# Attention's value product as fp32r parts: values' rounded and rest columns side by side as one 128-column operand, probabilities split in two

## The chip, the cores and the metric

The kernel runs on one core of a Trainium2 chip. The metric is the device time of one execution in microseconds (us), the median of three runs; smaller is better. The engines are PE (TensorE, matrix products), DVE (VectorE), ACT (ScalarE), POOL (GpSimd) and SP (SyncE, which issues the transfers). Each works through its own queue in order, and semaphores hold an instruction back until what it needs is there. SBUF is the memory on the chip, PSUM the memory that PE writes its products to.

## What is computed

The reference is two layers of a decoder trunk over 1024 positions with 1024 features, in fp32. A layer normalises its input, projects it, runs three groups of heads on the projection (sliding-window attention, an HGRN2 recurrence, a gated delta rule), projects their joined outputs, and then runs a SwiGLU feed-forward network (FFN). Each of the two halves of a layer is a residual that is scaled, shifted and gated by a modulation computed from a second input. Cut to the attention that the change touches:

```
kb, vb = band(k), band(v)          # this block of 128 positions and the one before
scores = jnp.einsum('bnqhgd,bnkhd->bnhgqk', qb, kb).astype(jnp.float32) * (d ** -0.5)
scores = jnp.where(valid[None, :, None, None], scores, -jnp.inf)   # causal, within 128 positions
m = jnp.maximum(scores.max(axis=-1, keepdims=True), sink)
p = jnp.exp(scores - m)
denom = p.sum(axis=-1, keepdims=True) + jnp.exp(sink - m)
out = jnp.einsum('bnhgqk,bnkhd->bnqhgd', (p / denom).astype(v.dtype), vb)
```

There are eight query heads in two groups that share a key and a value head each, with 64 features to a head.

## The kernel before

**Dense products.** All large products (input projection `p_fm` and `p_tm`, output projection `o_ps`, FFN `gu_ps` and `dn_ps`) go through `mm3`: both operands are split in a rounded part and a rest (`hhi`/`hlo`, `whi`/`wlo`), and three fp32r matmuls of 512 columns (256 for `p_tm`) make the product. They stream on PE nearly without a stop. For each weight piece a transfer lands, ACT rounds it (line 770) and DVE subtracts to get the rest (line 771). fp32r is the type of a matmul's operands that were rounded when written.

**Halves and mixers.** The 1024 positions are two halves of 512, each a sequence of four blocks of 128. A mixer is the work of the three head groups on one half of one layer: `gdn` (gated delta rule), `hgrn` and `attention`. They are Python generators, and `Weaver` takes the next step of the one that is least advanced. `Pace` puts such steps between the dense matmuls: each `mm3` ticks a clock, credit builds up at a rate, a step costs one credit, and a generator that yields a number is left alone until so many us of that clock have passed. So `yield 2.5` behind the probabilities' work says how much dense work shall stand between the transposes and the product. `end_m` runs whatever steps are left without a pause. Four mixers run: (layer 0, half 0) beside the projection of half 1, the three others beside FFN stages. Behind `end_m(0, 0)` comes the first output projection, which needs everything that the first mixer wrote.

**Attention in a block.** For each block, keys and queries are normalised, rotated, split and transposed (`pk`, `pq`). Then, for each of the two key/value heads g (a "group" here; 32 in all, 4 of them in a first block that has no block before it): eight score products `psc`, a softmax in `sc` (DVE lines 336 to 352, ACT lines 345 and 354), and four transposes that bring the probabilities to PSUM as `pt`. They are used twice: masked for this block as `ptc` and for the block before as `ptp` (POOL's affine_select, lines 360 and 364, which zeroes what lies outside the window), each behind an ACT copy from PSUM (lines 359 and 363). The value product is plain fp32:

```
og = po[64 * g:64 * g + 64].rearrange("p a b -> p (a b)")
T.matmul(og, k.vring[:, cur, 64 * g:64 * g + 64], ptc.rearrange("p a b -> p (a b)"),
         start=True, stop=first)
```

and the same on line 371 with `ptp` and the block before. `vring` holds the values of two blocks, copied by POOL on line 268. The profile names the slot of SBUF that `sc`, `ptc` and `ptp` lie in `scr`, and counts two records for each of these fp32 matmuls.

**The start.** `build_consts` fills mask constants (`mc`) on POOL in a scratch tile, and DVE casts them to `mcr` on line 101; `hgrn` uses them from its first block on. While they are made, the modulation's products run on DVE and POOL (lines 1172 and 1175, tile `adag`, with the tag "gt"), and the first pieces of the input projection begin on PE (`first_pieces`: `hhi` from ACT line 1150, `hlo` from DVE line 1151).

The scheduler of the framework sets the order of instructions on each engine from priorities and from when buffers come free, so a change of a few steps moves many rows.

## Time and profile before

| | us |
|---|---|
| median of 3 runs | 2741.18 (2739.95 to 2748.74) |
| the profiled execution | 2744.08 |
| its span in the profile | 2742.4 |
| PE busy | 2616.8 (95% of the span) |
| DVE busy | 1869.8 (68%) |
| ACT busy | 1158.3 (42%) |
| POOL busy | 377.9 (14%) |

The span is the time from the first to the last instruction of the profiled execution. An engine's share is an average over stages: where PE is busy throughout, the other engines' work is hidden; where it isn't, something else sets the time.

### The profile page before, as it was taken

The numbers are of one execution on the slowest core, as the hardware profiler recorded it, in microseconds if no ns is written. First come the engines' busy times: TensorE is split into PE (matmuls) and PEld (weight loads), VectorE is DVE, ScalarE is ACT, GpSimd is POOL, SyncE is SP. The second block draws the span as 40 slices with busy tenths as digits, with TensorE's granted clock in tenths as the row PEclk, the third lists the DMA queues.
The fourth block names the chain that finished last, engine by engine and source line by source line (L and its number), as shares of the span: only waits on it lengthen the run. The fifth ranks groups of instructions, "written<-read, shape, count | busy, mean of one in ns | idle before, by whom it ended". The sixth has DMA issues, their size and how long they took to land.

```text
span 2742.4 us, 42796 instructions
## 1 busy us (share of the span) xinstructions
PE 2616.8 (95%) x15488; PEld 2117.0 (77%) x15488; DVE 1869.8 (68%) x4863; ACT 1158.3 (42%) x2434; POOL 377.9 (14%) x560
## 2 busy tenths in 40 slices
PE   4989898899999999999999999999999999999999
PEld 3887776777777778887877777898787777788887
DVE  7679886777968567567887757637777854544444
ACT  4636573333445444433344444543344544322222
POOL 6132210402101001311011001211110100100000
PEclk9999999999999999999999999999999999999999
DMA  6644336543333355544433335452332224333323
GB/s 234 195 149 132 115 100 205 167 123 91 122 114 101 110 166 160 181 124 135 128 99 105 108 124 178 134 156 74 98 114 88 70 76 154 117 93 95 93 80 108
DMA packets 171956, 343.96 MB, mean 125 GB/s; under 512 B 20832, under 2 KB 80480, under 8 KB 171744
## 3 DMA queue, kind: packets, MB, share of 16 engines
q1 hardware_dynamic: 170880, 341.16, 40.0%
q8 instruction: 122, 2.00, 0.3%
q14 instruction: 90, 0.74, 0.1%
q10 hardware_dynamic: 864, 0.07, 0.0%
HBM read 299.15 MB, written 42.01 MB: 124 GB/s over the span
## 4 chain that ended last, share of the span: by engine, by line
PE 67%; DVE 17%; issue 5%; POOL 4%; ACT 4%; DMA 2%; SPq 0%; POOLq 0%; ACTq 0%; DVEq 0%
PE gu_ps L799 10%; PE gu_ps L800 9%; PE gu_ps L801 9%; PE dn_ps L799 5%; PE dn_ps L800 5%; PE dn_ps L801 5%; DVE wlo L771 3%; PE p_tm L800 2%; PE p_tm L801 2%; PE p_tm L799 2%; PE o_ps L800 2%; PE o_ps L801 2%; PE o_ps L799 2%; POOL n_xn L850 1%; PE pl L484 1%
## 5 line engine op out<-in xcount | busy, mean ns | idle before, releaser
L770 ACT ACTIVATE whi<-wraw 128x1024 fp32r<-128x1024 f32 (+3 forms) x484 | 422.9, 875 | 788.9 <-PE gu_ps L800 240.6
L771 DVE TENSOR_TENSOR wlo<-wraw,whi 128x1024 fp32r<-128x1024 f32 (+3 forms) x484 | 493.3, 1020 | 271.1 <-ACT whi L770 261.3
L799 PE MATMUL gu_ps<-hhi,whi 128*128 128x512 f32 x1408 | 572.4, 407 | 3.4 <-DVE n_xn L848 2.6
L800 PE MATMUL gu_ps<-hlo,whi 128*128 128x512 f32 x1408 | 559.8, 398 | 0.8 <-DVE hlo L852 0.7
L801 PE MATMUL gu_ps<-hhi,wlo 128*128 128x512 f32 x1408 | 560.2, 398 | 0.0
L799 PEld LDWEIGHTS gu_ps<-hhi,whi 128*128 128x128 f32 x1408 | 267.4, 190 | 74.0 <-issue 13.9
L801 PEld LDWEIGHTS gu_ps<-hhi,wlo 128*128 128x128 f32 x1408 | 266.1, 189 | 61.6 <-issue 0.8
L800 PEld LDWEIGHTS gu_ps<-hlo,whi 128*128 128x128 f32 x1408 | 266.6, 189 | 58.1 <-DVE hlo L852 2.8
L799 PE MATMUL dn_ps<-gt,whi 128*128 128x512 f32 x704 | 287.6, 410 | 2.0 <-DVE xt L1061 1.3
L800 PE MATMUL dn_ps<-gt,whi 128*128 128x512 f32 x704 | 278.5, 396 | 0.4 <-DVE gt L1049 0.4
L801 PE MATMUL dn_ps<-gt,wlo 128*128 128x512 f32 x704 | 277.5, 394 | 0.0
L799 PE MATMUL p_tm<-whi,hhi 128*128 128x256 f32 (+1 forms) x896 | 255.7, 286 | 6.7 <-ACT cx L875 3.5
L800 PE MATMUL p_tm<-wlo,hhi 128*128 128x256 f32 (+1 forms) x896 | 256.2, 286 | 5.8 <-DVE wlo L771 5.8
L801 PE MATMUL p_tm<-whi,hlo 128*128 128x256 f32 (+1 forms) x896 | 254.7, 284 | 0.0
L799 PEld LDWEIGHTS p_tm<-whi,hhi 128*128 128x128 f32 x896 | 170.3, 190 | 9.6 <-ACT cx L875 4.3
L800 PEld LDWEIGHTS p_tm<-wlo,hhi 128*128 128x128 f32 x896 | 170.3, 190 | 9.1 <-DVE wlo L771 7.5
L801 PEld LDWEIGHTS p_tm<-whi,hlo 128*128 128x128 f32 x896 | 170.1, 190 | 1.9 <-issue 1.6
L799 PEld LDWEIGHTS dn_ps<-gt,whi 128*128 128x128 f32 x704 | 132.3, 188 | 37.8 <-issue 7.6
L1061 DVE SCALAR_TENSOR_TENSOR xt<-dn_ps,gth,xt 128x512 f32<-128x512 f32 x144 | 107.8, 748 | 77.1 <-PE dn_ps L801 76.7
L801 PEld LDWEIGHTS dn_ps<-gt,wlo 128*128 128x128 f32 x704 | 132.3, 188 | 31.0
L800 PEld LDWEIGHTS dn_ps<-gt,whi 128*128 128x128 f32 x704 | 132.5, 188 | 30.6 <-DVE gt L1049 4.4
L1046 DVE TENSOR_TENSOR g_t<-g_t,gu_ps 128x512 f32<-128x512 f32 x88 | 60.2, 685 | 119.0 <-PE gu_ps L801 118.6
(409 smaller groups left out, 4436.3 us busy)
## 6 DMA issues: line engine op xcount, KB each, us to landing
wraw<-in_w_gate_dram SPq DMA_DIRECT2D x88, 512.0 KB, 3.7
wraw<-in_w_up_dram SPq DMA_DIRECT2D x88, 512.0 KB, 4.0
wraw<-in_ada_w_dram SPq DMA_DIRECT2D x80, 512.0 KB, 3.7
wraw<-in_w_down_dram SPq DMA_DIRECT2D x128, 256.0 KB, 2.7
wraw<-in_w_in_t_dram SPq DMA_DIRECT2D x48, 512.0 KB, 4.0
wraw<-in_w_in_f_dram SPq DMA_DIRECT2D x32, 512.0 KB, 4.0
wraw<-in_w_out_dram SPq DMA_DIRECT2D x32, 512.0 KB, 4.0
wraw<-in_w_down_dram SPq DMA_DIRECT2D x64, 192.0 KB, 2.4
```

Source lines behind the costliest of these rows:

```text
L484: T.matmul(pl[r][cols, li, p, :], lh, rh, start=True, stop=True)
L770: nc.scalar.activation(hi[:, 0:n], raw[:, 0:n], AF.Copy)
L771: nc.vector.tensor_tensor(out=lo[:, 0:n], in0=raw[:, 0:n], in1=hi[:, 0:n].bitcast(F32), op=ALU.subtract)
L799: T.matmul(out, lh, rh, start=first, stop=False)
L800: T.matmul(out, lh, rl, start=False, stop=False)
L801: T.matmul(out, ll, rh, start=False, stop=last)
L850: nc.gpsimd.tensor_scalar(out=xn, in0=xn, scalar1=acol[:, i:i + 1], scalar2=bcol[:, i:i + 1], op0=ALU.mult, op1=ALU.add)
L1046: V.tensor_tensor(out=t, in0=t, in1=pss[1], op=ALU.mult)
L1061: V.scalar_tensor_tensor(out=x, in0=ps, scalar=k.gth[l][:, m:m + 1], in1=x, op0=ALU.mult, op1=ALU.add)
```

## The change

Values are kept twice, as their rounded part (ACT copy) and the rest (DVE subtraction), side by side: for a head, `vring[:, cur, g]` has 2 x 64 columns. Probabilities likewise: `ptc[:, 0]` is the rounded copy that ACT makes from PSUM, `ptc[:, 1]` what DVE leaves by subtracting it. POOL masks both parts for both blocks, four selects where there were two (two for one in a first block). The product is four fp32r matmuls (two in a first block) that add up in one PSUM tile `po`, whose upper 64 rows belong to the rounded values and whose lower 64 to the rest; an ACT copy and a DVE addition join them into the output tile `a_ot`. Further: `po` is taken for each group rather than for both, `yield 2.5` becomes `yield 4.5`, a `yield 1.0` follows the products and a `yield 0.0` goes; attention's input tile is single, and the next block's transfer is issued behind the normalisation. To make room, the slots of scratch are handed out in halves (class `Slot`, `half`), `hgrn`'s `h_ld` is cut to half and its first half lies in such a half slot, and the mask constants' scratch is a tile of the pool `gp` with the tag "gt", taken behind the first step of `build_consts`.

```diff
@@ -66,9 +66,7 @@
     nc, tc = k.nc, k.tc
     cp = k.const
     G, V = nc.gpsimd, nc.vector
-    t1 = k.mp.tile([128, 1024], F32, name="h_ld")
     t2 = k.mp.tile([128, 6, 128], F32, name="cv").rearrange("p a t -> p (a t)")
-    mc = t1.rearrange("p (l t) -> p l t", l=NL + 1)
     idt = t2[:, 640:768]
     mk, mk2 = t2[:, 0:128], t2[:, 128:192]
     e, ef = t2[:, 192:320].bitcast(I32), t2[:, 320:448]
@@ -83,6 +81,7 @@
     k.ones = cp.tile([128, 128], F32, name="ones")
     G.memset(k.ones, 1.0)
     yield
+    mc = k.gp.tile([128, 1024], F32, name="mct", tag="gt").rearrange("p (l t) -> p l t", l=NL + 1)
 
     def sel(ap, pattern, base, cm):
         G.affine_select(out=ap, in_=ap, pattern=pattern, compare_op=ALU.is_ge, fill=0.0,
@@ -189,7 +188,7 @@
         nc.scalar.activation(k.sin2[:, :, j, :], ang, AF.Sin)
         nc.scalar.activation(k.cos2[:, :, j, :], nn, AF.Sin)
     k.kring = cp.tile([128, 4, 2, 128], F32R, name="kring")
-    k.vring = cp.tile([128, 2, 128], F32, name="vring")
+    k.vring = cp.tile([128, 2, 2, 2, 64], F32R, name="vring")
     k.sB = cp.tile([128, 2, 128], F32, name="sB")
     k.sC = cp.tile([128, 2, 128], F32, name="sC")
 
@@ -246,26 +245,25 @@
     qs = mp.tile([128, 4, 2, 64], F32R, name="a_qs")
     qT = mp.tile([128, 4, 128], F32R, name="a_qT")
     ks = mp.tile([128, 2, 2, 2, 64], F32R, name="a_ks")
-    sc = r2[:, 1024:1536].rearrange("p (a t) -> p a t", a=4)
-    ptc = r2[:, 1536:2048].rearrange("p (a t) -> p a t", a=4)
-    ptp = r2[:, 2048:2560].rearrange("p (a t) -> p a t", a=4)
-    qk = r2[:, 0:640].rearrange("p (h d) -> p h d", d=64)
+    r2, pf = r2
+    at = r2[:, 0:768]
+    qk = r2[:, 768:1408].rearrange("p (h d) -> p h d", d=64)
+    sc = r2[:, 1408:1920].rearrange("p (a t) -> p a t", a=4)
+    ptc, ptp = (pf[:, 2 * i:2 * i + 2].rearrange("p u (a t) -> p u a t", a=4) for i in range(2))
     sq = mp.tile([128, 10, 64], F32, name="a_sq")
     def load(b):
-        at = r2[:, 2560 + 768 * (b % 2):3328 + 768 * (b % 2)]
         nc.sync.dma_start(out=at, in_=tmr[b, :, 0:768])
-        return at
-
-    nxt = load(0)
+
+    load(0)
     yield 3.0
     for b in range(NB):
         gb = NB * h + b
         cur = gb % 2
         first = gb == 0
-        at = nxt
-        if b + 1 < NB:
-            nxt = load(b + 1)
-        G.tensor_copy(k.vring[:, cur, :], at[:, 640:768])
+        av = at[:, 640:768].rearrange("p (g d) -> p g d", g=2)
+        A.activation(k.vring[:, cur, :, 0, :], av, AF.Copy)
+        V.tensor_tensor(out=k.vring[:, cur, :, 1, :], in0=av, in1=k.vring[:, cur, :, 0, :].bitcast(F32),
+                        op=ALU.subtract)
         a3 = at[:, 0:640].rearrange("p (h d) -> p h d", d=64)
         A.activation(sq, a3, AF.Square)
         ss = k.small.tile([128, 10], F32, name="a_ss")
@@ -280,6 +278,8 @@
             V.scalar_tensor_tensor(out=qk[:, 8 + j, :], in0=a3[:, 8 + j, :],
                                    scalar=rs[:, 8 + j:9 + j], in1=lc.gq[:, 1, :],
                                    op0=ALU.mult, op1=ALU.mult)
+        if b + 1 < NB:
+            load(b + 1)
         xr = qk[:, :, 0:16]
         pc = sq[:, 0:3, :].rearrange("p a d -> p (a d)")[:, 0:160].rearrange("p (h d) -> p h d", d=16)
         ps_ = sq[:, 3:6, :].rearrange("p a d -> p (a d)")[:, 0:160].rearrange("p (h d) -> p h d", d=16)
@@ -308,7 +308,7 @@
         A.activation(k.kring[:, :, cur, :], pk, AF.Copy)
         den = k.small.tile([128, 8], F32, name="a_den")
         yield 0.5
-        po = k.pb.tile([128, 4, 128], F32, name="po", tag="b")
+        ot = mp.tile([128, 4, 128], F32, name="a_ot", tag="fo")
         for g in range(2):
             pq = k.pb.tile([128, 4, 128], F32R, name="pq", tag="b")
             for j in range(4):
@@ -356,24 +356,26 @@
             pt = k.pb.tile([128, 4, 128], F32, name="pt", tag="b")
             for j in range(4):
                 T.transpose(pt[:, j, :], sc[:, j, :], k.ident)
-            A.activation(ptc, pt, AF.Copy)
-            G.affine_select(out=ptc, in_=ptc, pattern=[[0, 4], [1, 128]],
-                            compare_op=ALU.is_ge, fill=0.0, base=0, channel_multiplier=-1)
-            if not first:
-                A.activation(ptp, pt, AF.Copy)
-                G.affine_select(out=ptp, in_=ptp, pattern=[[0, 4], [-1, 128]],
-                                compare_op=ALU.is_gt, fill=0.0, base=0, channel_multiplier=1)
-            yield 2.5
-            og = po[64 * g:64 * g + 64].rearrange("p a b -> p (a b)")
-            T.matmul(og, k.vring[:, cur, 64 * g:64 * g + 64], ptc.rearrange("p a b -> p (a b)"),
-                     start=True, stop=first)
-            if not first:
-                T.matmul(og, k.vring[:, 1 - cur, 64 * g:64 * g + 64],
-                         ptp.rearrange("p a b -> p (a b)"), start=False, stop=True)
-            if g == 0:
-                yield 0.0
-        ot = mp.tile([128, 4, 128], F32, name="a_ot", tag="fo")
-        A.activation(ot, po, AF.Copy)
+            A.activation(ptc[:, 0], pt, AF.Copy)
+            V.tensor_tensor(out=ptc[:, 1], in0=pt, in1=ptc[:, 0].bitcast(F32), op=ALU.subtract)
+            for u in range(2):
+                pu = ptc[:, u].bitcast(F32)
+                if not first:
+                    G.affine_select(out=ptp[:, u], in_=pu, pattern=[[0, 4], [-1, 128]],
+                                    compare_op=ALU.is_gt, fill=0.0, base=0, channel_multiplier=1)
+                G.affine_select(out=ptc[:, u], in_=pu, pattern=[[0, 4], [1, 128]],
+                                compare_op=ALU.is_ge, fill=0.0, base=0, channel_multiplier=-1)
+            yield 4.5
+            po = k.pb.tile([128, 4, 128], F32, name="po", tag="b")
+            pof = po.rearrange("p a b -> p (a b)")
+            terms = [(v, t, u) for v, t in ((cur, ptc), (1 - cur, ptp))[:1 if first else 2] for u in range(2)]
+            for i, (v, t, u) in enumerate(terms):
+                T.matmul(pof, k.vring[:, v, g].rearrange("p a b -> p (a b)"), t[:, u].rearrange("p a b -> p (a b)"),
+                         start=(i == 0), stop=(i == len(terms) - 1))
+            yield 1.0
+            rows = slice(64 * g, 64 * g + 64)
+            A.activation(ot[rows], po[0:64], AF.Copy)
+            V.tensor_tensor(out=ot[rows], in0=ot[rows], in1=po[64:128], op=ALU.add)
         nc.sync.dma_start(out=mixr[:, 0:4, 128 * b:128 * b + 128], in_=ot)
         yield 0.0
 
@@ -419,24 +421,25 @@
     V, A, G, T = nc.vector, nc.scalar, nc.gpsimd, nc.tensor
     tmr = src.tm.rearrange("(b p) c -> p b c", p=128)
     mixr = src.mix.rearrange("(a p) t -> p a t", p=128)
...
-    ld = mp.tile([128, 1024], F32, name="h_ld")
-    kk, lf, vv, gate = (ld[:, 256 * i:256 * i + 256] for i in range(4))
+    lk = r2[1][:, 1536:2048]
+    ld = mp.tile([128, 512], F32, name="h_ld")
+    kk, lf, vv, gate = (t[:, 256 * i:256 * i + 256] for t in (lk, ld) for i in range(2))
 
     def load(b):
-        nc.sync.dma_start(out=ld[:, 0:512], in_=tmr[:, b, C_KK:C_KK + 512])
+        nc.sync.dma_start(out=lk, in_=tmr[:, b, C_KK:C_KK + 512])
 
     load(0)
     yield 3.0
     for b in range(NB):
-        nc.sync.dma_start(out=ld[:, 512:1024], in_=tmr[:, b, C_BV:C_BV + 512])
+        nc.sync.dma_start(out=ld, in_=tmr[:, b, C_BV:C_BV + 512])
         nc.sync.dma_start(out=qT, in_=src.bq.rearrange("(a p) t -> p a t", p=128)[:, :, 128 * b:128 * b + 128])
         lfh = mp.tile([128, 256], F32R, name="h_lfh")
         A.activation(lfh, lf, AF.Copy)
@@ -806,8 +809,24 @@
     return k.stg.tile([128, 512], F32, name=name, tag="stg")
 
 
+class Slot:
+    def __init__(self, halves):
+        self.halves = halves
+
+    def __getitem__(self, key):
+        p, i, c = key
+        return self.halves[i // 4][p, i % 4, c]
+
+    def flat(self):
+        return [t.rearrange("p a t -> p (a t)") for t in self.halves]
+
+
+def half(k, which, j, name, dt=F32):
+    return k.act.tile([128, 4, HT], dt, name=name, tag=f"{which}{j}")
+
+
 def slot(k, which, name, dt=F32R):
-    return k.act.tile([128, 8, HT], dt, name=name, tag=which)
+    return Slot([half(k, which, j, f"{name}{j}", dt) for j in range(2)])
 
 
 class Norm:
...
@@ -1365,20 +1384,21 @@
         return act(lambda: x_load(k, sts[(0, 1)], 1, f))
 
     def scr(which):
-        t = slot(k, which, "scr", F32).rearrange("p a t -> p (a t)")
-        return t
+        return lambda: slot(k, which, "scr", F32).flat()
+
+    def atn(which):
+        return lambda: (half(k, which, 0, "sca").rearrange("p a t -> p (a t)"), half(k, which, 1, "scp", F32R))
 
...
-            s.wv = Weaver([(gdn(k, lc, h, s.dst, quart(r1)), N_C),
-                           (chain(lambda: hgrn(k, lc, l, h, s.dst, r2),
-                                  lambda: attention(k, lc, h, s.dst, r2)), N_A + N_B)])
+            s.wv = Weaver([(gdn(k, lc, h, s.dst, quart(scr("hi" + which)())), N_C),
+                           (chain(lambda: hgrn(k, lc, l, h, s.dst, scr("lo" + which)()),
+                                  lambda: attention(k, lc, h, s.dst, atn("lo" + which)())), N_A + N_B)])
         return act(fn)
 
...
```

Three places show how this moves instructions. The first is the start. On DVE before, the cast of the masks stands among the squares of the norm (`n_acc`) at the head of the queue, and further on come the last low halves `hlo` with the modulation's products (`adag`) around them:

```order
L1121 TENSOR_TENSOR mod_90<-mod_90,adab_91 128x2
L101 CAST mcr<-h_ld 128x1024
L825 TENSOR_TENSOR n_acc<-n_acc,n_sq 128x512
...
L1175 SCALAR_TENSOR_TENSOR adag,mod_90<-adag,cond 128x1024
L163 CAST cv<-cv 128x8
L1121 TENSOR_TENSOR mod_90<-mod_90,adab_91 128x2
L166 TENSOR_TENSOR cv<-cv 128x64
L1122 SCALAR_TENSOR_TENSOR am_96<-mod_90,gain_93 128x1
L1151 TENSOR_TENSOR hlo<-n_xn,hhi 128x512
```

After, the cast stands behind the modulation's last product here, ahead of the last two `hlo`:

```order
L1194 SCALAR_TENSOR_TENSOR adag,mod_90<-adag,cond 128x1024
L100 CAST mcr<-mct 128x1024
L1139 TENSOR_TENSOR mod_90<-mod_90,adab_91 128x2
L1170 TENSOR_TENSOR hlo_235<-n_xn,hhi_233 128x512
L1140 SCALAR_TENSOR_TENSOR am_96<-mod_90,gain_93 128x1
L102 COPY tri<-mct 128x128
...
L774 TENSOR_TENSOR wlo<-wraw,whi 128x1056
L179 SCALAR_TENSOR_TENSOR cv<-cv 128x64 x3
L774 TENSOR_TENSOR wlo<-wraw,whi 128x1056
L1170 TENSOR_TENSOR hlo_235<-n_xn,hhi_233 128x512
```

POOL in the changed kernel fills the masks behind its last modulation product, where the kernel before fills them right behind its first constants:

```order
L141 MEMSET cv 128x128
L87 AFFINE_SELECT cv<-cv 128x128
L1191 TENSOR_TENSOR adag<-adag,cond 128x1024
L90 MEMSET mct 128x1024
L87 AFFINE_SELECT mct<-mct 128x64 x2
...
L87 AFFINE_SELECT mct<-mct 128x64 x2
L549 MEMSET scg 128x512
```

So the cast, and with it the two `hlo`, moved behind POOL's whole mask work. The second place is the end of the first mixer on PE. Before, the last dense matmul (`p_tm`) is followed by one group's product, one whole group, and the output projection `o_ps`:

```order
L801 MATMUL p_tm<-whi,hlo 128x256
...
L368 MATMUL po<-scr,vring 64x512
L371 MATMUL po<-scr,vring 64x512
L315 MATMUL pq<-identr,a_qs 128x128 x4
L602 MATMUL pv<-identr,cv 128x128 x2
L331 MATMUL psc<-kring,a_qT 128x256 x8
...
L358 MATMUL pt<-identr,scr 128x128 x3
...
L368 MATMUL po<-scr,vring 64x512
L454 MATMUL pd<-mcr,h_lfl 128x512
L371 MATMUL po<-scr,vring 64x512
...
L799 MATMUL o_ps<-mhi,whi 128x512 x3
```

After, the last dense matmul is followed by the products of the fifth group (left out here) and by the transposes and products of three more:

```order
L804 MATMUL p_tm<-whi,hlo_1790 128x256
...
L358 MATMUL pt<-identr,sca 128x128 x3
...
L373 MATMUL po<-scp,vring 128x512 x4
...
L307 MATMUL pk<-identr,a_ks 128x128 x4
L315 MATMUL pq<-identr,a_qs 128x128 x4
...
L331 MATMUL psc<-kring,a_qT 128x256 x8
L358 MATMUL pt<-identr,sca 128x128 x4
L373 MATMUL po<-scp,vring 128x512
...
L373 MATMUL po<-scp,vring 128x512 x3
L331 MATMUL psc<-kring,a_qT 128x256 x8
L358 MATMUL pt<-identr,sca 128x128 x4
L373 MATMUL po<-scp,vring 128x512 x4
L802 MATMUL o_ps<-mhi_4984,whi 128x512 x3
```

Three groups' transposes now stand behind the last `p_tm`, where one group's stood. The third place is a group in an FFN stage, again on PE. Before, it reads, from the transposes to the products:

```order
L358 MATMUL pt<-identr,scr 128x128 x4
L799 MATMUL gu_ps<-hhi,whi 128x512
L800 MATMUL gu_ps<-hlo,whi 128x512
L801 MATMUL gu_ps<-hhi,wlo 128x512
...
L801 MATMUL gu_ps<-hhi,wlo 128x512
L368 MATMUL po<-scr,vring 64x512
L371 MATMUL po<-scr,vring 64x512
L799 MATMUL gu_ps<-hhi,whi 128x512
```

with 15 dense matmuls in between. After, there are 18 in between, and the two products are four matmuls:

```order
L358 MATMUL pt<-identr,sca 128x128 x4
L802 MATMUL gu_ps<-hhi_5624,whi 128x512
L803 MATMUL gu_ps<-hlo_5626,whi 128x512
L804 MATMUL gu_ps<-hhi_5624,wlo 128x512
...
L804 MATMUL gu_ps<-hhi_5625,wlo 128x512
L373 MATMUL po<-scp,vring 128x512 x4
L802 MATMUL gu_ps<-hhi_5625,whi 128x512
```

The products moved back by three dense matmuls here, and took the shape of their neighbours.

## Rows read from the trace of the kernel before

**Rows 1.** The page, its head (PE matmul, PEld weight load, DVE VectorE, POOL GpSimd)
```profile
span 2742.4 us, 42796 instructions
...
PE 2616.8 (95%) x15488; PEld 2117.0 (77%) x15488; DVE 1869.8 (68%) x4863; ACT 1158.3 (42%) x2434; POOL 377.9 (14%) x560
```

**Rows 2.** Table of stretches: length, busy us by engine, granted clock, DMA
```profile
200.00:330.00 130.00, 117.19 (x944) 96.11 (x945) 118.16 (x441) 74.94 (x206) 26.12 (x51) 0.95 0.37 116
...
360.00:400.00 40.00, 36.73 (x337) 29.46 (x337) 33.47 (x135) 27.38 (x68) 5.41 (x10) 1.00 0.42 136
400.00:430.00 30.00, 20.77 (x121) 12.94 (x117) 17.28 (x49) 17.69 (x57) 3.41 (x5) 0.83 0.50 161
```

**Rows 3.** Timeline of PE in an FFN stage: start us, length, engine, line
```profile
2196.91 0.39 PE L800 MATMUL dn_ps<-gt,whi 128*128 128x512 f32 x1
2197.14 0.39 PE L801 MATMUL dn_ps<-gt,wlo 128*128 128x512 f32 x1
2197.46 1.07 PE L368 MATMUL po<-scr,vring 128*64 128x512 f32 x2
...
2199.32 0.50 PE L799 MATMUL dn_ps<-gt,whi 128*128 128x512 f32 x1
2199.66 0.39 PE L800 MATMUL dn_ps<-gt,whi 128*128 128x512 f32 x1
```

**Rows 4.** Groups of instructions: line, count, total busy us, mean ns, idle before them
```profile
L771 DVE TENSOR_TENSOR wlo<-wraw,whi 128x1024 fp32r<-128x1024 f32 x284 | 359.5, 1267 | 221.6 <-ACT whi L770 212.6 <-DMA cb<-tm 3.8
...
L1046 DVE TENSOR_TENSOR g_t<-g_t,gu_ps 128x512 f32<-128x512 f32 x88 | 60.2, 685 | 119.0 <-PE gu_ps L801 118.6
...
L368 PE MATMUL po<-scr,vring 128*64 128x512 f32 x64 | 35.2, 632 | 4.1 <-POOL scr L360 3.9
...
L371 PE MATMUL po<-scr,vring 128*64 128x512 f32 x56 | 29.4, 608 | 0.0
...
L360 POOL TENSOR_SCALAR_AFFINE_SELECT scr<-scr 128x512 f32<-128x512 f32 x32 | 25.3, 789 | 456.8 <-ACT scr L359 431.5 <-PE gu_ps L801 25.1
...
L359 ACT ACTIVATE scr<-pt 128x512 f32<-128x512 f32 x32 | 19.1, 596 | 20.9 <-PE pt L358 20.6
...
L364 POOL TENSOR_SCALAR_AFFINE_SELECT scr<-scr 128x512 f32<-128x512 f32 x28 | 18.3, 654 | 0.4 <-ACT scr L363 0.4
```

**Rows 5.** Timeline of POOL, a select that stands behind gdn work
```profile
830.81 1.62 POOL L360 TENSOR_SCALAR_AFFINE_SELECT scr<-scr 128x512 f32<-128x512 f32 x1
```

**Rows 6.** Timeline of POOL at the start
```profile
1.42 0.95 POOL L91 MEMSET h_ld<- 128x1024 f32 x1
...
2.46 12.08 POOL L88 TENSOR_SCALAR_AFFINE_SELECT h_ld<-h_ld 128x64 f32<-128x64 f32 x29
...
60.98 0.53 POOL L546 MEMSET scg<- 128x512 f32 x1 [4.83 <-DVE adag L1175]
```

**Rows 7.** Timeline of DVE at the start
```profile
14.86 0.68 DVE L101 CAST mcr<-h_ld 128x1024 fp32r<-128x1024 f32 x1
...
64.54 0.69 DVE L1151 TENSOR_TENSOR hlo<-n_xn,hhi 128x512 fp32r<-128x512 f32 x1
```

**Rows 8.** Timeline of PE in the first projection
```profile
58.77 0.63 PE L801 MATMUL p_fm<-hhi,wfl 128*128 128x512 f32 x1
...
61.33 0.63 PE L799 MATMUL p_fm<-hhi,whi 128*128 128x512 f32 x1
...
68.80 0.40 PE L800 MATMUL p_fm<-hlo,wfh 128*128 128x512 f32 x1
```

**Rows 9.** Timeline of PE ahead of the first output projection
```profile
359.39 0.38 PE L358 MATMUL pt<-identr,scr 128*128 128x128 f32 x2
...
406.81 0.28 PE L801 MATMUL p_tm<-whi,hlo 128*128 128x256 f32 x1
...
419.96 1.06 PE L358 MATMUL pt<-identr,scr 128*128 128x128 f32 x3 [5.79 <-ACT scr L354]
...
428.94 0.91 PE L799 MATMUL o_ps<-mhi,whi 128*128 128x512 f32 x3
```

26 lines of the change are left out of this document (12 added, 14 removed).

## Prediction

> **What bounds the kernel now.** I read the page's head first. TensorE (PE) is busy for 95% of the span, VectorE (DVE) for 68%, ScalarE (ACT) for 42% and GpSimd (POOL) for 14% [rows 1]. Only some 126 us of the span are without PE work, so a saving on PE is a saving of time wherever PE is the bound. The table of stretches shows where it isn't: from 200 to 330 us PE is busy 117.2 of 130 us beside a DVE that is busy 118.2, and from 400 to 430 us only 20.8 of 30, at a mean granted clock of 0.83 [rows 2]. That last stretch is the drain of the first mixer, which the first output projection waits for. The profiled execution took 2744.1 us (span 2742.4), 2.9 more than the median; I make the sum against 2744.1 and take 2.9 off at its end. A change of 0.3%, 8.2 us, is about what this kernel's measurement can tell from none, so "same" means 2733 to 2749.
>
> **The value product itself.** Before, each of the 32 groups (four blocks, two key/value heads, two halves, two layers) has a matmul on line 368 and all but four have one on line 371, both plain fp32. A neighbourhood in an FFN stage shows their price: the fp32r matmuls beside them step by 0.23 us (2196.91 to 2197.14), so 2197.37 is when line 368 could have been followed by the next fp32r one, and that one, which starts at 2199.32, is followed by its neighbour after 0.34. From 2197.37 to 2199.43 is 2.06 us for the pair [rows 3]. After, a full group has four fp32r matmuls of 512 columns and 128 weight columns, the same shape as those neighbours: 4 x 0.233 = 0.93. The saving is 1.13 us in a full group. A first-block group goes from 1.03 to 0.47, saving 0.56. The FFN stages hold 22 full groups and 2 first ones: -24.9 - 1.1 = **-26 us**. The remaining 6 and 2 are in the first mixer, which is counted below.
>
> **Probabilities.** A group had two ACT copies (596 ns each) and two POOL selects (789 and 654 ns) [rows 4]. It now has one ACT copy, one DVE subtraction that reads PSUM (priced as line 1046's, 685 ns [rows 4]), and four selects. The chain from the last transpose to the last select is 0.38 (transposes [rows 9]) + 0.1 + 0.60 + two selects of the rounded part 1.28 (beside which the subtraction's 0.69 lies) + two of the rest 1.28 = 3.6 us; 4.3 where a hand-over or the subtraction is late. The second product needs the fourth select. The order rows give it time: 18 dense matmuls stand between transposes and products of nearly all these groups, 18 x 0.233 = 4.2 us, where before there were 9 to 18 and the first product needed one copy and one select. So there is little margin, and it goes where DVE or POOL is occupied: a select took 1.62 us once behind gdn's POOL work [rows 5], and a weight subtraction on DVE takes 1.27 [rows 4]. Before, PE waited 3.9 us in all for the first select [rows 4]. I take 0.15 us in each of the 24 groups, **+3.5 us**; bounds are 0, if 18 rows cover all, and 1.2 each (29 us), if every group has two selects as long as the 1.62 one, less the 0.7 of margin that the likely chain leaves.
>
> The Trainium skill speaks against this part: SBUF — State Buffer, "SBUF: two separate sides", has one port pair shared by DVE and GpSimd as an exclusive lock that is held for a whole instruction when a DVE operation has two SBUF inputs. By that rule a select meeting a weight subtraction waits for all of it. The trace bears the rule out in part, with a mean first select of 789 against 654 for the one behind it; by the rule alone, at every select, the sum would be that of the second rival.
>
> **Values, output and scratch.** The POOL copy of values goes; an ACT copy and a small DVE subtraction come, once for each of 16 blocks, a block ahead of their use. The output's DVE addition and ACT copy for each head stand behind the product, where nothing on PE waits but the tile's next use, a group later. DVE gets some 45 us in all, in stages where it is idle for a third of the time: 0 on the path, up to 2 us if one product's bank comes free late. The later load of the next attention block has a whole block to land: 0.
>
> **Start.** The mask constants' scratch moves from a tile of its own time to one that shares its buffers with the weight products of the modulation ("gt"). Before, POOL fills it from 1.42 us on: a memset of 0.95 and 29 selects of 12.08 [rows 6], and DVE casts it at 14.86 in 0.68 [rows 7]. After, the memset is queued behind POOL's fourth product and waits for the DVE product of the buffer's last holder, as line 546's memset did before, which began at 60.98 [rows 6]. So the masks end at 60.98 + 0.95 + 12.08 = 74.0. The order rows put DVE's cast of them ahead of the last two low halves of the first projection's input, the first of which ran at 64.54 [rows 7]. That one is then done at 74.0 + 0.68 + 0.1 + 0.6 = 75.4, and PE, which in order needs it at 68.80 [rows 8], stands still for 6.7 us. Earlier in this stage PE ran seven matmuls at a step of 0.43 instead of 0.23 (from 58.77, the last at 61.33 [rows 8]), which cost 1.4; behind this longer gap I take nine, +1.8. Together **+8.5 us**, and PE's stages follow on each other from there. Bounds: 0, if the memset finds its buffer free earlier, and 11, if the second low half is late again behind two weight subtractions.
>
> **The first mixer's end.** Here 915 matmul rows (in units of 512 columns) of projections are woven with eight attention groups by a planner that spends credit and waits out each step's stated latency. The latency goes from 2.5 to 4.5 and a step of 1.0 is added, so the groups slide back: the transposes of the fifth group stand behind 910 of the 915 rows, before behind 836. From these transposes to the first output projection before took 428.94 - 359.39 = 69.6 us, the last dense matmul at 406.81 and 22.1 us of drain behind it, of which 5.8 were a wait for one softmax [rows 9]. In the order after, three whole groups and the fifth's product stand behind the last dense row. The transposes move back by 74 x 0.233 = 17.2 us, less some 2 to 5 that the four groups ahead of them save and that rows brought forward into PE's idle time (12.8 us between 200 and 330 [rows 2]) regain: to 372 to 377. What then follows has 1.2 us of dense rows for 18.4, but the same softmax chains and DVE work: DVE was busy 33.5 of 40 and 17.3 of 30 us there [rows 2], 51, to which four groups' additions bring 6, so at least 57; at most the old 70. Half way, 63 from 374.5, gives 437.5, **+9 us** with this stage's own saving in it. Ends: 429 (0) and 447 (+18); -4, if the idle time takes nearly all the dense rows, and +23, if the drain's PE work runs at the low clock throughout. The other three mixers' last products stand a good hundred matmuls ahead of theirs, before and after, so no drain is added there.
>
> **Sum.** 2744.1 - 26 + 3.5 + 8.5 + 9 = 2739.1; less 2.9, **2736 us**, a gain that a measurement hardly tells from none.
>
> **The rivals.**
> *The drain costs nothing* (0.27). The dense rows that moved forward fill PE's idle 12.8 us, and the first mixer ends 4 us earlier: 2736 - 13 = 2723; 2715 if the start's stall isn't there either. For it: PE had idle time ahead. Against it: DVE was as busy as PE in that stretch.
> *The four selects become the wait* (0.15; the side on which it is slower). Without any wait the sum is 2732.6, so from 0.7 us in each of the 24 groups on it is slower by over 0.3%; at 1.2 us, 2761. For it: twice the selects in one chain, the 1.62 us row. Against it: 634 to 654 ns are usual, and 18 rows of cover.
> *The drain in full* (0.12). Everything at +18 to +23: 2745 to 2750, the same or just slower. For it: chains of one engine after another, low clock. Against it: less work in between.
> *The fp32r products aren't cheaper* (0.04). At a step of 0.43 a group costs 1.72, and the 26 shrink to 8: 2754. Against it: the same shape beside it runs at 0.23.
> *My forecast* (0.38) has 2728 to 2745 as its own range; the last 0.04 is for what I don't see.
>
> The cases give faster 0.38 (the first rival and a quarter of the forecast's own range, with a little of the rest), same 0.40, slower 0.22 (the selects, the fp32r step, part of the full drain). Eight in ten lie from 2716, where the drain and the start both cost nothing, to 2760, where the selects do.
>
> **What would show it.** Line 373's products step by 0.23; the FFN stages shorten by about 1.1 us a group; waits of po for POOL total 7 to 8 us. The masks' last select ends near 74, with the cast behind it and a PE gap from about 69 to 75. The first output projection starts near 446 (428.9 + 8.5 + 9), with 30 to 40 us of thin PE work ahead. It is wrong if that start is under 430 or over 460, if the gap isn't there, or if po waits over 0.7 us a group.

## The result, and the profile after

The changed kernel takes 2779.57 us (median of four runs, 2777.38 to 2780.58) against 2744.64 for the kernel before in the runs beside it: 1.0127 times its time, 95% interval 1.0111 to 1.0142. It is slower by some 35 us, where a gain of 5 was forecast, and it lies outside the forecast's range of 2716 to 2760. The profiled execution took 2777.38 us, its span 2775.6. PE is busy for 2612.8 us in it, 4.0 less than before [rows 1].

Three starts divide a run into the same dense work in both kernels: the first `p_tm` (the start is over), the first `o_ps` (the first mixer is over) and the first `gu_ps`, from which the FFN stages and what lies between them run to the end. In the kernel before they are at 75.5, 428.9 and 512.4 us of 2742.4. After, by tile, with the least, median and greatest ns and the first and last start:

```profile
L802 PE MATMUL p_tm<-whi,hhi x896: 274/283/683, 82.6 to 1874.0; 128*128 128x256 f32 x154, 128*128 128x264 f32 x26
...
L802 PE MATMUL o_ps<-mhi,whi x256: 387/393/797, 463.8 to 2377.6; 128*128 128x512 f32 x128
...
L802 PE MATMUL gu_ps<-hhi,whi x1408: 387/393/776, 548.9 to 2753.8; 128*128 128x512 f32 x176
```

So the start is 7.1 us longer; from `p_tm` to `gu_ps` it is 466.3 us against 436.9, 29.4 longer, of which 27.8 lie ahead of the first `o_ps`, the end that the forecast's +9 is for; from `gu_ps` to the end 2226.7 against 2230.0, 3.3 shorter. Against the forecast of +8.5, +9 and -22.5 the start is right, and the other two are not.

**The start.** What answers to [rows 6], POOL's timeline after:

```profile
59.36 0.96 POOL L90 MEMSET mct<- 128x1024 f32 x1 [3.68 <-DVE adag L1194]
60.39 10.54 POOL L87 TENSOR_SCALAR_AFFINE_SELECT mct<-mct 128x64 f32<-128x64 f32 x29
```

To [rows 7], DVE's:

```profile
70.96 1.45 DVE L100 CAST mcr<-mct 128x1024 fp32r<-128x1024 f32 x1 [8.46 <-POOL mct L87]
...
72.40 0.68 DVE L1170 TENSOR_TENSOR hlo<-n_xn,hhi 128x512 fp32r<-128x512 f32 x1
```

And to [rows 8], PE's:

```profile
73.13 0.80 PE L803 MATMUL p_fm<-hlo,wfh 128*128 128x512 f32 x1 [7.33 <-DVE hlo L1170]
...
77.14 0.63 PE L803 MATMUL p_fm<-hlo,wfh 128*128 128x512 f32 x1
77.57 0.63 PE L804 MATMUL p_fm<-hhi,wfl 128*128 128x512 f32 x1
```

The masks end at 70.9 rather than 74.0, since the modulation's product was earlier and the selects took 10.5 us. DVE idled 8.46 us for them, the cast took 1.45, the low half ended at 73.1, and PE stood still for 7.33 us. Then it ran at a step of 0.43 until 78.9, twelve matmuls for the forecast's nine.

**The end of the first mixer.** What answers to [rows 2], the table of stretches after, with one stretch more:

```profile
200.00:330.00 130.00, 119.26 (x991) 102.25 (x991) 114.34 (x412) 70.52 (x191) 28.46 (x51) 0.95 0.38 120
360.00:400.00 40.00, 35.88 (x294) 30.44 (x293) 34.93 (x137) 24.91 (x61) 10.56 (x13) 1.00 0.49 149
400.00:430.00 30.00, 20.93 (x215) 16.71 (x213) 23.03 (x92) 11.82 (x53) 5.24 (x9) 0.66 0.20 62
430.00:460.00 30.00, 11.73 (x43) 8.71 (x43) 11.77 (x41) 13.33 (x40) 4.27 (x7) 0.57 0.23 66
```

And to [rows 9], PE's timeline:

```profile
387.95 0.33 PE L358 MATMUL pt<-identr,sca 128*128 128x128 f32 x1
...
391.32 0.28 PE L804 MATMUL p_tm<-whi,hlo 128*128 128x256 f32 x1
...
410.20 1.06 PE L358 MATMUL pt<-identr,sca 128*128 128x128 f32 x3 [4.75 <-ACT sca L354]
...
422.46 2.07 PE L373 MATMUL po<-scp,vring 128*128 128x512 f32 x4
...
442.19 1.36 PE L358 MATMUL pt<-identr,sca 128*128 128x128 f32 x4 [5.32 <-ACT sca L354]
445.86 0.79 PE L373 MATMUL po<-scp,vring 128*128 128x512 f32 x1 [2.31 <-POOL scp L366]
...
455.89 1.35 PE L358 MATMUL pt<-identr,sca 128*128 128x128 f32 x4 [5.39 <-ACT sca L354]
...
463.83 1.65 PE L802 MATMUL o_ps<-mhi,whi 128*128 128x512 f32 x3 [1.33 <-ACT mhi L1226]
```

The last dense matmul starts at 391.32, 15.5 us earlier than before although the start was 7.1 later. The dense rows didn't fill PE's idle time, though. From the first `p_tm` to the last, before and after:

```profile
75.50:406.81 331.31, 303.82 (x2514) 261.50 (x2514) 276.74 (x939) 195.33 (x466) 71.24 (x112) 0.97 0.43 135
82.60:391.32 308.72, 280.88 (x2254) 248.63 (x2253) 260.05 (x852) 174.32 (x393) 70.72 (x103) 0.97 0.45 142
```

PE is idle there for 27.8 us, before for 27.5; its work fell by 22.9, as the mixer's work moved behind the dense rows. Behind the last of them lie 72.5 us (before 22.1) in which three groups of attention, with blocks of the two other head groups, go through their chains one step after another. PE is busy for 20.9 and 11.7 of 30 us there, and the granted clock is 0.66 and 0.57 of full speed, so most of the time at the lower of its two levels, 0.50. A group's four products, 0.93 us at full clock (below), take 1.87 from 422.46 to the next instruction of PE, at 424.33.

**A group in an FFN stage.** What answers to [rows 3], PE's timeline after:

```profile
2201.71 0.40 PE L804 MATMUL gu_ps<-hhi,wlo 128*128 128x512 f32 x1
2201.95 1.09 PE L373 MATMUL po<-scp,vring 128*128 128x512 f32 x4
2202.88 0.39 PE L802 MATMUL gu_ps<-hhi,whi 128*128 128x512 f32 x1
2203.11 0.40 PE L803 MATMUL gu_ps<-hlo,whi 128*128 128x512 f32 x1
```

PE's waits after, from the first `gu_ps` to the end: for which line, total us, times, the longest:

```profile
PE g_p L669 <- DVE g_qkT L666: 19.6, 9, 3.5
PE pl L487 <- DVE scr L501: 6.0, 4, 1.7
...
PE po L373 <- POOL scp L366: 4.9, 6, 1.7
PE dn_ps L802 <- ACT gt L1067: 3.1, 7, 1.0
...
PE pt L358 <- ACT sca L354: 1.6, 1, 1.6
```

The same view of before, from 512.4 on:

```profile
PE g_p L666 <- DVE g_qkT L663: 13.6, 8, 3.5
...
PE pl L484 <- DVE scr L498: 2.3, 1, 2.3
PE po L368 <- POOL scr L360: 1.9, 2, 1.7
```

Four products take 0.93 us, and the dense matmuls beside them go on at 0.23: the products cost what was forecast. PE's waits for `po` are 4.9 us, against 1.9 before. But `g_p`, `pl`, `dn_ps` (0.7 before) and `pt`, which the change doesn't touch, wait longer too. Before has 3.2 us of `g_p` waits for POOL besides, which are gone after, so `g_p` as a whole waits some 3 us longer.

### The profile page after: what moved, and what is told of

It is laid out like the page before. It is cut to its first block, busy times and chain, and to the rows that moved or that the text cites. A ratio compares the mean times of both kernels' runs of the same rounds, so it can differ in the third digit from the quotient of the medians.

```text
span 2775.6 us, 42989 instructions
## 1 busy us (share of the span) xinstructions
PE 2612.8 (94%) x15488; PEld 2150.6 (77%) x15488; DVE 1925.9 (69%) x4943; ACT 1157.8 (42%) x2437; POOL 412.7 (15%) x604
```

## The experiments

Each run has three numbers beside its time: the start up to the first `p_tm`, the mixer from there to the first `gu_ps`, and the FFN stages from there to the end of its profiled execution, by the same rows as above, each as the difference from the profiled execution of before. Of the mixer's number, the column behind it gives the part up to the first `o_ps`; the rest is the output projection and what follows it up to `gu_ps`. Single executions scatter: three kernels that are the same up to there (e6, e7 and e9, the first three runs with fp32 in the first mixer) gave 436.6, 437.1 and 443.0 us for the mixer, so 6 us there are no finding. In the last column e5 and e6, whose FFN stages have the same code, differ by 6.5, so there too a difference of that size is read only where the medians show it as well.

| run | us, median | ratio to before, 95% interval | start | mixer | of it to `o_ps` | FFN stages |
|---|---|---|---|---|---|---|
| changed kernel | 2779.57 | 1.0111 to 1.0142 | +7.1 | +29.4 | +27.8 | -3.3 |
| e1 early masks | 2768.66 | 1.0069 to 1.0107 | -2.2 | +34.2 | +32.3 | -6.6 |
| e2 short yields | 2755.28 | 1.0032 to 1.0063 | +6.6 | +18.4 | +10.9 | -16.6 |
| e3 latencies alone, in before | 2773.09 | 1.0099 to 1.0130 | -0.2 | +27.4 | +27.3 | +0.3 |
| e4 old product in the new layout | 2754.05 | 1.0027 to 1.0057 | +6.8 | +2.0 | +1.8 | -0.7 |
| e5 early masks, steps of before | 2753.63 | 1.0032 to 1.0060 | -1.9 | +18.3 | +14.3 | -6.4 |
| e6 as e5, fp32 in the first mixer | 2733.26 | 0.9955 to 0.9980 | -0.3 | -0.3 | -0.1 | -12.9 |
| e7 as e6, steps of the change | 2738.39 | 0.9980 to 0.9999 | -0.5 | +0.2 | +0.2 | -6.1 |
| e8 rounded probabilities only | 2752.16 | 1.0026 to 1.0052 | +7.1 | +22.3 | +18.8 | -28.2 |
| e9 as e6, rounded products first | 2734.68 | 0.9944 to 0.9972 | -0.3 | +6.1 | +2.9 | -15.5 |
| e10 as e5, rounded probabilities only | 2736.15 | 0.9956 to 0.9983 | -1.4 | +27.3 | +13.6 | -23.4 |
| e11 as e5, join per block | 2747.09 | 1.0014 to 1.0043 | -1.9 | +13.0 | +10.4 | -11.5 |
| e12 as e5, no rest of values | 2745.37 | 0.9996 to 1.0018 | -0.2 | +15.3 | +12.1 | -10.9 |
| e13 as e6, work beside the chain | 2755.19 | 1.0030 to 1.0066 | -1.8 | +17.7 | +12.0 | -13.3 |
| e14 as e6, chain alone | 2737.13 | 0.9971 to 0.9993 | -1.9 | +6.0 | +5.7 | -13.3 |

**The masks.** Two tiles that are free at the start take the scratch (levels 0 to 3 and 4 to 7), and the rest of the changed kernel stays:

```diff
-    mc = k.gp.tile([128, 1024], F32, name="mct", tag="gt").rearrange("p (l t) -> p l t", l=NL + 1)
+    mcs = [k.mp.tile([128, 4, 128], F32, name="mca", tag="h_ld"), k.mp.tile([128, 4, 128], F32, name="mcb", tag="fo")]
```

> The changed kernel, but with the mask constants' scratch in two tiles of 512 columns that are free at the start, so that POOL fills them at once as before. Theory (the masks' late buffer costs the start's 7 us and everything behind is only shifted): first p_tm at 75.5 instead of 82.6, first output projection at about 457 instead of 463.8, time about 2772.5. Rival (the 7 us would be made up or lost elsewhere, since the first mixer's end hangs on DVE's chains): output projection still near 464, time 2779.

The time fell by 10.9 to 2768.66, and the first `p_tm` starts at 73.3. So the start's loss comes from where the masks stand, and little of it was made up or lost later. In the profile the first `o_ps` starts at 459.0, nearer to the theory's 457 than to the rival's 464. (The mixer's 4.8 more and the FFN stages' 3.3 less are within the scatter of one execution.)

**The stated latencies.** Two runs from opposite sides, one taking the change's steps out of the changed kernel, one putting nothing but them into the kernel before:

```diff
-            yield 4.5
+            yield 2.5
...
-            yield 1.0
```

> The changed kernel, but with the planner's stated latencies of before (2.5 behind the transposes, no step of its own behind the products). Theory (the stated latencies push the first mixer's groups behind the last dense row; the work itself hardly matters): drain ahead of the first output projection back to 20 to 30 us, that projection at about 436; but the products come after some 12 to 15 dense matmuls where the selects want 16 to 18, so po waits rise by up to 10 us in the FFN stages: time 2752 to 2762. Rival (the additional DVE, ACT and POOL work makes the drain): projection still at 455 to 465, time 2780 to 2790.

```diff
-            yield 2.5
+            yield 4.5
...
-            if g == 0:
-                yield 0.0
+            yield 1.0
```

> The kernel before, with nothing of the change but the planner's steps (4.5 in place of 2.5, and a step of 1.0 behind each group's products). Theory (stated latencies make the drain): first output projection at 448 to 458 instead of 428.9, FFN stages as before, time 2763 to 2773. Rival (the change's additional work makes it): projection at 429 to 433, time 2745 to 2748.

Latencies alone bring the kernel before to 1.0114 times its time: 2773.09. Its stretches, as above:

```profile
400.00:430.00 30.00, 19.03 (x186) 13.87 (x185) 19.39 (x69) 11.23 (x39) 1.91 (x4) 0.72 0.55 163
430.00:460.00 30.00, 18.77 (x51) 9.54 (x52) 5.82 (x16) 11.37 (x32) 2.44 (x4) 0.60 0.14 39
```

And its `o_ps`, by tile:

```profile
L798 PE MATMUL o_ps<-mhi,whi x256: 388/393/797, 456.0 to 2372.3; 128*128 128x512 f32 x128
```

The projection waits until 456.0 with no additional work on any engine. So the rival fell for this run. In the changed kernel, though, short yields gave back 16.9 of the 27.8 up to the projection, not the whole: it starts at 446.4, between the two expectations. So the two causes don't add up: the latencies alone make 27.3 us (e3), the additional work at short steps 10.9 (e2; 14.3 in e5 below), and both together 27.8, or 32.3 with early masks (e1). The short yields also show the price of less cover in the FFN stages: po's waits rise from 4.9 to 14.0 us, and still these stages take 13 us less in its profile than with the change's steps. (A second such pair, e5 below against e1, shows no gain there: -6.4 and -6.6.)

**Layout.** The changed kernel with the fp32 product, its two selects and its steps put back, but all halves, the later `hgrn` and the late masks kept:

```diff
-            A.activation(ptc[:, 0], pt, AF.Copy)
-            V.tensor_tensor(out=ptc[:, 1], in0=pt, in1=ptc[:, 0].bitcast(F32), op=ALU.subtract)
+            A.activation(ptc, pt, AF.Copy)
+            G.affine_select(out=ptc, in_=ptc, pattern=[[0, 4], [1, 128]],
+                            compare_op=ALU.is_ge, fill=0.0, base=0, channel_multiplier=-1)
...
```

> The changed kernel's layout (halves of slots, hgrn's later start, single attention input, late masks) with the fp32 product, the selects, the copies and the stated latencies of before. Theory (layout costs only the start's 7 us): first p_tm at 82.6, output projection at about 436 to 440, FFN stages as before, time about 2752. Rival (the layout itself, hgrn's later start above all, makes the drain): projection at 455 or later, time 2770 or more.

2754.05: the start's 6.8 and next to nothing else. The layout costs nothing that can be told from the scatter, but for the masks.

**Where the parts pay.** With early masks, the steps of before are restored exactly (2.5, none behind the products, 0.0 between a block's groups), which puts the groups of the FFN stages at the dense matmuls they had; then the first mixer alone (`old`) goes back to fp32; then that one gets the change's steps in its FFN stages:

```diff
+            if g == 0:
+                yield 0.0
```

> The changed kernel with early masks and with all of the planner's steps as before (2.5 behind the transposes, the step of 0.0 between the two groups of a block, no step behind the products), so that the groups stand in the FFN stages at the same dense matmuls as before. If the FFN stages lost their gain by the stated latencies, they now take 14 to 18 us less than before in all, in spite of some 14 us of po waits. The first mixer should cost 8 to 17 more than before (its additional work in a stretch where PE isn't the bound): time 2735 to 2745. Rival (the additional work on DVE, ACT and POOL eats the FFN gain whatever the steps): FFN stages within 5 of before, time 2750 or more.

```diff
+            if old:
+                A.activation(oc, pt, AF.Copy)
+                G.affine_select(out=oc, in_=oc, pattern=[[0, 4], [1, 128]],
+                                compare_op=ALU.is_ge, fill=0.0, base=0, channel_multiplier=-1)
...
```

> As the run with the steps of before and early masks, but the first mixer (layer 0, half 0) keeps the fp32 product with its two selects, and only the three mixers beside FFN stages use the parts. Theory (the parts pay where PE is the bound and cost where DVE and the chains are): first mixer within 3 us of before, FFN stages 14 to 18 less, time 2727 to 2734, faster than both kernels. Rival (a gain in the FFN stages is an accident of one order): time 2740 to 2746.

> As the run with fp32 in the first mixer, but with the changed kernel's own steps (4.5 and 1.0) in the FFN stages. Theory (the stated latencies cost the FFN stages most of their gain): FFN stages only 2 to 6 us less than before, time 2739 to 2744. Rival (they don't, the losses there came in with the late first mixer): time as with the steps of before, 2727 to 2734.

The first missed: 2753.63, as the mixer was still 18.3 us longer at its old steps, and the FFN stages gained 6.4 in its profile, less than the 14 to 18 expected. The second came out at 2733.26, faster than the changed kernel and, by an interval of 0.9955 to 0.9980, than the kernel before; its FFN stages gained 12.9, a little less than expected. Its stretches, to be held against [rows 2]:

```profile
400.00:430.00 30.00, 18.67 (x108) 11.93 (x108) 15.18 (x46) 17.42 (x56) 2.84 (x5) 0.83 0.47 153
511.80:2728.90 2217.10, 2160.30 (x12316) 1756.98 (x12316) 1498.00 (x3722) 890.65 (x1855) 278.59 (x364) 1.00 0.38 118
```

From its first `gu_ps` to its end the changed kernel has:

```profile
548.90:2775.60 2226.70, 2168.87 (x12316) 1769.34 (x12316) 1508.85 (x3722) 889.71 (x1855) 276.44 (x364) 0.99 0.38 117
```

And the kernel before:

```profile
512.40:2742.40 2230.00, 2182.28 (x12310) 1750.90 (x12310) 1464.32 (x3661) 890.23 (x1852) 249.20 (x331) 0.99 0.38 117
```

In e6 the drain is as before, and from the first `gu_ps` on PE is busy 2160.3 us, 8.6 less than the changed kernel's 2168.9, for the same matmuls, at a mean clock of 1.00 rather than 0.99. The change's steps in the same kernel cost 5.1 us: 2738.39, just under the theory's 2739 to 2744. Of the waits that the changed kernel showed above, `g_p` (18.4 us), `pl` (6.4) and `dn_ps` for ACT (4.4) are back with them, where the run with the steps of before has 12.4 for `g_p` (and 3.2 for POOL), 1.5 for `pl` and no such wait for `dn_ps`; `po` falls from 13.6 to 4.7 in exchange. They belong to the order that the latencies make. An example from the changed kernel, on PE's timeline:

```profile
1230.28 0.39 PE L492 MATMUL pl<-scr 64*64 64x64 f32 x4
...
1232.49 1.46 PE L487 MATMUL pl<-scr 64*64 64x64 f32 x24 [1.39 <-DVE scr L501]
```

On DVE's:

```profile
1230.85 0.75 DVE L617 TENSOR_TENSOR scr<-pa,g_rr 128x256 f32<-128x256 f32 x2
1231.51 0.42 DVE L626 TENSOR_TENSOR g_qd<-scr,eg 128x256 f32<-128x256 f32 x1
1231.85 0.70 DVE L501 COPY_PREDICATED scr<-lmask,pl 128x128 f32<-128x128 uint8 x3
```

And in the table of stretches:

```profile
1229.00:1232.00 3.00, 2.10 (x32) 1.37 (x30) 2.90 (x17) 1.06 (x2) 0.32 (x1) 1.00 0.57 175
1232.00:1235.00 3.00, 2.51 (x30) 2.33 (x31) 3.00 (x6) 0.90 (x2) 1.55 (x3) 0.60 0.00 0
1235.00:1238.00 3.00, 3.00 (x9) 2.33 (x8) 1.43 (x7) 0.00 (x0) 0.40 (x1) 0.50 0.57 175
```

`hgrn`'s chain of levels (`pl`, line 501) meets `gdn`'s operations (lines 617 and 626) in DVE's queue, PE waits 1.39 us behind a string of small matmuls and one dense one, and from 1232 to 1238 the clock is mostly at its lower level.

**The additional work.** Six runs look for what costs 18 us in the mixer at the steps of before, 14.3 of them ahead of the first `o_ps`. Two leave the rest of the probabilities out, with the change's steps and with those of before:

```diff
-            V.tensor_tensor(out=ptc[:, 1], in0=pt, in1=ptc[:, 0].bitcast(F32), op=ALU.subtract)
-            for u in range(2):
+            for u in range(1):
```

> The changed kernel without the rest part of the probabilities (left out: the DVE subtraction, two of the four selects, two of the four products), steps and masks as changed. If the stated latencies push the first mixer's groups back, its projection still starts at 450 or later, and the time is 2758 to 2768 (11 us less on PE in the FFN stages). If the additional selects and the subtraction make the drain, the projection starts at 435 to 440 and the time is 2735 to 2742.

> As the run with early masks and the steps of before, in all mixers with parts, but without the rest part of the probabilities (left out: DVE subtraction, two selects, two products a group). In that run the first mixer ended 18 us later than before at the same stated latencies. If the rest's selects and subtraction in the chain make this, the first mixer is now within 6 of before, and with 25 to 30 less in the FFN stages the time is 2714 to 2724. If the other additions do (split values, the output's addition, products a group apart), it is still 12 to 18 late: 2726 to 2736.

With the change's steps the projection still starts at 454.8: latencies. The time, 2752.16, is 6 us under the range that went with this, as the FFN stages fell by 24.9 against the changed kernel's. The two products left out are 22 x 0.47 + 2 x 0.23 = 10.8 of that; the other 14 would be the subtraction's and the selects'. With the steps of before the FFN stages fell by only 17.0 against e5's, which leaves 6 for them, so their price there is 6 to 14 us. The time of that run, 2736.15, is at the upper end of its second expectation, and its executions scatter from 2729.5 to 2746.7 (the profile is of the slowest). Up to the projection it is 13.6 us late where e5 is 14.3: the rest of the probabilities isn't what delays the first mixer. Two more move or remove operations on values and output:

```diff
-            A.activation(ot[rows], po[0:64], AF.Copy)
-            V.tensor_tensor(out=ot[rows], in0=ot[rows], in1=po[64:128], op=ALU.add)
+            pos.append(po)
```

> As the run with early masks and the steps of before (2753.6), but a group's output is joined (ACT copy, DVE addition) behind both groups of a block instead of behind each. If the joins stand at the head of ACT's and DVE's queues while PE hasn't finished, and the first mixer's 18 us come from that, most of it goes: 2738 to 2745. If not, it stays within 4: 2750 to 2757.

```diff
-        V.tensor_tensor(out=k.vring[:, cur, :, 1, :], in0=av, in1=k.vring[:, cur, :, 0, :].bitcast(F32),
-                        op=ALU.subtract)
...
-            V.tensor_tensor(out=ot[rows], in0=ot[rows], in1=po[64:128], op=ALU.add)
```

> As the run with early masks and the steps of before, without the rest of the values (left out: the DVE subtraction of a block, the DVE addition of a group, half the weight columns); the products on PE take the same time, the four selects stay. If DVE's additional operations on values and output make the first mixer's 18 us, most of it goes: 2735 to 2743. If the chain of copy, subtraction and four selects makes them, 2748 to 2755.

Both fell between their expectations: 6.5 and 8.3 less than e5, neither the whole, and only 3.9 and 2.2 of that lie ahead of the projection, little to be told from the scatter. So a last pair added to e6, whose first mixer is undisturbed, either the work without the chain or the chain without the other work:

```diff
+                V.tensor_scalar(out=px[0], in0=pt, scalar1=1.0, scalar2=0.0, op0=ALU.mult, op1=ALU.add)
+                for j in range(1 if first else 2):
+                    G.affine_select(out=px[1], in_=px[0], pattern=[[0, 4], [1, 128]],
...
+                A.activation(ot[rows], po[rows], AF.Copy)
+                V.tensor_scalar(out=ot[rows], in0=ot[rows], scalar1=1.0, scalar2=0.0, op0=ALU.mult, op1=ALU.add)
```

> The run with fp32 in the first mixer (2733.3), where the first mixer now also does the parts' additional work, but with no product waiting for it: a DVE pass over the transposes' PSUM tile and two selects a group that nothing uses, the split of every block's values (ACT, DVE), an ACT copy and a DVE pass (times 1.0) over the output of each group. If occupied engines make the first mixer's 18 us, it ends 10 to 18 later than there: 2743 to 2751. If only the longer chain ahead of the products does, 2732 to 2737.

```diff
+                V.tensor_tensor(out=px[0], in0=pt, in1=oc, op=ALU.subtract)
+                for j in range(1 if first else 2):
+                    G.affine_select(out=px[1], in_=px[0], pattern=[[0, 4], [1, 128]],
+                                    compare_op=ALU.is_ge, fill=0.0, base=0, channel_multiplier=-1)
```

> The run with fp32 in the first mixer, where each group's chain ahead of the products is as long as with the parts: behind the first ACT copy a DVE subtraction and two selects that nothing uses stand in front of the selects that the products wait for. No additional work on values or output. If the chain makes the 18 us: 2743 to 2751. If it is the work on DVE and ACT around it: 2733 to 2738.

Work beside the chain: 2755.19 (2744.95 to 2764.94), 22 us over e6. Chain alone: 2737.13, 4 over. A stretch of the first, whose profile is of one of its faster executions, 2746.73:

```profile
330.00:400.00 70.00, 57.96 (x463) 46.75 (x463) 59.50 (x229) 47.53 (x109) 18.32 (x31) 0.93 0.34 111
```

The same of e6:

```profile
330.00:400.00 70.00, 66.26 (x634) 53.77 (x633) 61.47 (x257) 48.66 (x121) 15.18 (x25) 1.00 0.37 116
```

From 330 to 400 us PE does 58.0 us of work where e6 does 66.3, at a clock of 0.93 for 1.00, though no product waits for any of the additions. So occupied engines are enough to delay this mixer by about as much as e5 was late, and the longer chain alone, with its subtraction and selects, isn't. How they do it stays open: DVE isn't busier in this stretch, 59.5 us for 61.5. Nor is it shown that e5 lost its time in the same way. The last dense matmul, the transposes behind it and the projection in e5:

```profile
403.15 0.28 PE L807 MATMUL p_tm<-whi,hlo 128*128 128x256 f32 x1
...
417.90 1.35 PE L360 MATMUL pt<-identr,sca 128*128 128x128 f32 x4 [0.90 <-ACT sca L356]
...
433.33 1.36 PE L360 MATMUL pt<-identr,sca 128*128 128x128 f32 x4 [6.99 <-ACT sca L356]
...
441.26 1.65 PE L805 MATMUL o_ps<-mhi,whi 128*128 128x512 f32 x3 [1.33 <-ACT mhi L1229]
```

And the first and the last of these in e13:

```profile
417.56 0.28 PE L842 MATMUL p_tm<-whi,hlo 128*128 128x256 f32 x1
...
439.13 0.96 PE L840 MATMUL o_ps<-mhi,whi 128*128 128x512 f32 x3 [1.33 <-ACT mhi L1264]
```

In e13 the dense rows end late and the drain is 21.6 us, as before. In e5 they end early and the drain is 38.1, with the transposes of two groups behind them where before and e13 have one. And PE's waits for `po` ahead of the projection are 9.6 us in e5 against 3.7 in e6, so the chain of selects may have a part in e5's delay.

**The order of the products.** One run tried to gain more in the FFN stages:

```diff
-            terms = [(v, t, u) for v, t in ((cur, ptc), (1 - cur, ptp))[:1 if first else 2] for u in range(2)]
+            terms = [(v, t, u) for u in range(2) for v, t in ((cur, ptc), (1 - cur, ptp))[:1 if first else 2]]
```

> As the run with fp32 in the first mixer and the steps of before, but the four products of a group run in the order of the selects: both that use the rounded probabilities first, both that use the rest behind them. Theory (po's waits there, about 14 us, are for the third and fourth select): PE has two products of 0.23 to run while these end, up to 0.47 in each of some 18 waiting groups, waits down to 6 to 9 us, time 2726 to 2731. Rival (the first product waits already, for the ACT copy and the first selects, or the fourth select ends last anyway with nothing gained): 2731 to 2736.

The rival held: 2734.68, the same as e6 (the intervals overlap).

## Why the prediction was wrong, step by step

**The products: right.** A full group's four products take 0.93 us for the pair's 2.06, as worked out.

**The selects' waits: right in size.** They were put at +3.5 us; `po` waits rose from 1.9 to 4.9 us in the FFN stages. The longer latencies bought that (14.0 in e2 without them). The rival of the four selects, which needed 0.7 us a group, didn't decide it.

**The start: right.** +8.5 forecast, +7.1 measured, by the mechanism that was named; e1 takes it away again. That the size fits is in part luck: the masks ended 3 us earlier than worked out, and PE came to the low half 3 us earlier too.

**"The first mixer's end", +9: wrong by 19 us.** It measured +27.8, and the projection started at 463.8, over the 460 that was named as a sign of being wrong. The groups slid as the order rows said, and the fifth group's transposes came at 387.95, or 380.9 without the start's 7.1, for the forecast's 374.5: 6 of the 19 us. Idle time of PE was to win some of that slide back, and it didn't shrink. The step that failed is "Half way, 63 from 374.5": with fewer dense rows behind it, the chain to the projection was taken to get shorter. It got longer, 463.83 - 387.95 = 75.9 us, over the "at most the old 70": the other 13.

Two things make that delay, each shown by runs of its own. The stated latencies space the steps in the planner's order and leave three groups for the drain (e3 has +27.3 with no other edit), and in this drain the granted clock is at 0.57 to 0.66, which the working had kept for the far end of the range. And the parts' work on DVE, ACT and POOL delays the projection at the steps of before too (e5 +14.3, e13 +12.0), and 4 to 6 us more are lost behind its start, where the granted clock is 0.97 and 0.98 for 1.00 before. This contradicts the placing of the values' and the output's operations at "0 on the path" in this stretch. That DVE had 118 us of work in 130 there [rows 2] may be the reason; it isn't shown. e4 clears the layout. How the 18 us divide among the joins, the values' parts and the chain stays open; e11 and e12 take 6.5 and 8.3 off the whole time, and leaving out the rest of the probabilities takes nothing off this stage that can be told from the scatter.

**"FFN stages, -26 and +3.5": wrong by 19 us.** The mechanism was right and its gain was given back beside it. The table of stretches shows how: from the first `gu_ps` on, the changed kernel's PE is busy 2168.9 us and idle 57.8, where before it was busy 2182.3 and idle 47.7. Busy time fell by 13.4 rather than 26, so the other matmuls took some 13 longer (from 1232 to 1238 the stretches show such a place, at the lower clock), and idle time rose by 10.1 rather than 3.5, of which `po` is 3. That the products themselves give the saving is seen in e6, where busy time fell by 22.0. The forecast put all further work on ACT, DVE and POOL at "0 on the path, up to 2". e8 and e10 show 14 and 6 us for the subtraction and the two selects of the rest, and e7 against e6 shows 5.1 for the change's steps. These may overlap, and how the 19 us divide stays open.

**The chances.** The rival "the drain in full" (0.12) was the right case in kind, at +18 to +23; with +28 for it and next to no FFN gain, the time lay 20 us outside the range. The range's upper end took one such case at a time, but the same edits, latencies and additional operations, stand behind both.

**The long selects.** The 1.62 us select of [rows 5], at 830.81, isn't explained by `gdn`'s work on POOL ahead of it, as the prediction reads it. A weight subtraction on DVE had begun before it, and the select ended 0.5 us after that one's end:

```profile
830.34 1.60 DVE L771 TENSOR_TENSOR wlo<-wraw,whi 128x1024 fp32r<-128x1024 f32 x1
```

Of the eight selects (of 60) that took over 0.9 us in the kernel before, seven began during such a subtraction; the eighth ran beside another operation of DVE with two inputs in SBUF. The Trainium skill's rule that was weighed (SBUF — State Buffer, "SBUF: two separate sides") was not what decided: chain and selects alone cost 4 us in e14. The trace agrees with the rule itself in these eight selects.
